# mLSTM head norm as a per-chunk factor and offset on ScalarE, and the first convolution tap on ScalarE

## The chip, the cores and the metric

The kernel runs on one core of one Trainium2 chip. The metric is the device time of one execution in microseconds (us); lower is better. A core has five engines with a queue each: PE (TensorE, matrix products), DVE (VectorE), ACT (ScalarE), POOL (GpSimd) and SP (SyncE, which here only issues transfers). Each engine takes its queue strictly in order, and an instruction that waits holds up everything behind it.

## The reference, cut to what matters

One layer over 1024 tokens of width 1024: differential attention and an mLSTM side by side, sigmoid gates, a gated MLP, a final norm. The change lies in the mLSTM branch, four heads of 128 channels:

```python
qk_m = jax.nn.silu(causal_dwconv(qk_m, conv_m_w[i]))           # 4 taps per channel
qm, km = jnp.split(qk_m, 2, axis=-1)
...
h = num / jnp.maximum(jnp.abs(den), jnp.exp(-m_t))[..., None]   # mLSTM output per token
...
def head_layernorm(x, g):
    mu = jnp.mean(xf, axis=-1, keepdims=True)
    var = jnp.mean(jnp.square(xf - mu), axis=-1, keepdims=True)
    return (xf - mu) * lax.rsqrt(var + EPS) * g
hm = head_layernorm(hm, ml_norm_g[i]) * jax.nn.sigmoid(om)
```

## The kernel before, in words

Features lie on the 128 partitions and tokens in the free dimension, except inside an mLSTM head, where tokens are on partitions. Float32 accuracy comes from splitting each operand into a high and a low part (`split`, L119 to L126: ACT writes `wh`, DVE writes `wl`), so each product is three matmuls of 128x512 (L374, L375, L376).

The large projections run as pairs through `products` (L366): seven blocks, in the order B11, T1, T2, B21, T3, B22, T4, of 12 matmuls each. Three PSUM banks serve a pair: b2 takes B11, T2, T3 and T4, b3 takes T1 and B22, b4 takes B21. `c_blocks` (L787) copies the bank after B11, T1 and T2 to SBUF on ACT (`copy`, L295) and adds in the later blocks on DVE (`tt`, L292). So T3 may not write b2 before ACT has copied T2's sum out of it (the copy named `u2`).

The stage of the mLSTM heads alternates pairs of projections with the work of a head:

- `make_qk(h)` (L800) computes query and key of a head and runs the four-tap convolution per half of 512 tokens in `conv_silu` (L804): the first tap on DVE (L807), three more taps by DVE (L810, and L813 for the few columns that reach into the other half), a sigmoid on ACT (L816), a product on DVE (L292 or L820).
- `mlstm_head(h)` (L855) forms scores (`pS`, L877) and transposed keys (`pk`, L878) from query and key, multiplies by decay weights on DVE (`xb`, L292, and `kw`, L880), and steps through eight chunks of 128 tokens: `pn` (L888, L890) into `num` by ACT (L891), and the state `C` by `pc` (L894) and DVE (L899).
- The head norm then works on `num`, 128 partitions x 8 chunks x 128 channels (a 129th column is the denominator): `rd` is the reciprocal of the denominator (L907 to L909), `mu` minus the mean (L910, L911). Three DVE passes over all 1024 columns add `mu` (L912), multiply by `rd` (L915) and multiply by the root (L921). Between them ACT squares each chunk and sums it (L918, an activation and a read of the accumulator per chunk), DVE scales the sums (L919) and POOL raises them to the power of minus a half (L920).
- `mlstm_out` (L925) runs the next pair of projections (`gate_pair`) and transposes `num` on PE (`pt`, L932, eight matmuls), which DVE multiplies into the output gate (`om`, L934). After the last head, SP loads the outputs of heads 0 to 2 back (`hml`, L541) and ACT and DVE split them.

The order of the instructions on each engine's queue is not that of the code: when the program is built, a scheduler places them by its own estimates of cost. The heads' work is therefore mixed with the products of the pairs, and a changed instruction can move others.

Of the kernel before, what the change touches and what calls it, by code (L numbers as in the profile page):

```python
# [13 lines left out]
AF = mybir.ActivationFunctionType  # L14
ALU = mybir.AluOpType
# [4 lines left out]
P = 128  # L20
# [4 lines left out]
NTB = S // P  # L25
# [44 lines left out]
def block_kernel(ctx: ExitStack, tc: tile.TileContext, a: dict, out: bass.AP):  # L70
    nc = tc.nc
    PE, ACT, DVE, POOL, SP = nc.tensor, nc.scalar, nc.vector, nc.gpsimd, nc.sync
# [25 lines left out]
    def v(name, i=0, n=1):  # L98
        lo = _VEC_COLS[name][0] + i
        return vec[:, lo:lo + n]  # L100

    def acc(name):
        return pools["acc"].tile([P, HALF], F32, tag="acc", name=name)

    def mid(name):
        if "mid" not in pools:
            return acc(name)
        return pools["mid"].tile([P, HALF], F32, tag="mid", name=name)
# [4 lines left out]
    def half_slice(half):  # L113
        return slice(half * HALF, (half + 1) * HALF)
# [81 lines left out]
    with tc.tile_pool(name="ld", bufs=3) as ld:  # L196

        ss = [ld.tile([P, S], F32, tag=f"ss{q}", name="ss1", bufs=1) for q in range(2)]
        for k in range(KD):
# [10 lines left out]
            else:  # L210
                DVE.tensor_scalar(out=hi, in0=xt, scalar1=v("g1", k), scalar2=None, op0=ALU.mult)
            DVE.scalar_tensor_tensor(out=lo, in0=xt, scalar=v("g1", k), in1=hi.bitcast(F32),
                                     op0=ALU.mult, op1=ALU.subtract)
# [77 lines left out]
    def tt(eng, out, in0, in1, op):  # L291
        eng.tensor_tensor(out=out, in0=in0, in1=in1, op=op)  # L292

    def copy(out, ps):
        ACT.activation(out=out, in_=ps, func=AF.Copy)  # L295
# [485 lines left out]
    def work(name, w=S, dtype=F32):  # L781
        return mw.tile([P, w], dtype, tag="m", name=name)

    def s_tile(tag, bufs=1):
        return mw.tile([P, HALF], F32, tag=tag, name=tag, bufs=bufs)

    def c_blocks(blocks, ready):  # L787

        s1, u2, s5 = s_tile("s1"), s_tile("u2"), s_tile("s5")
        for blk, ps in products(blocks):  # L790
            if blk in ("B11", "T1", "T2"):
                copy({"B11": s1, "T1": s5, "T2": u2}[blk], ps)
            elif blk == "T4":
                ready(1, 0, ps)
            else:
                t, row, half = {"B21": (s1, 0, 0), "T3": (s5, 1, 1), "B22": (u2, 0, 1)}[blk]
                tt(DVE, t, ps, t, ALU.add)
                ready(row, half, t)

    def make_qk(h):  # L800
        cvs = [mw.tile([P, S], F32, tag="cv", name="cv", bufs=3) for _ in range(2)]
        z = {}

        def conv_silu(row, half, prev):  # L804
            o, zt = cvs[row][:, half_slice(half)], z[row, half]
            i = h + 4 * row
            DVE.tensor_scalar(out=o, in0=zt, scalar1=v("cm", i * 4 + 3), scalar2=None, op0=ALU.mult)  # L807
            for j in (2, 1, 0):
                d, w = 3 - j, v("cm", i * 4 + j)
                DVE.scalar_tensor_tensor(out=o[:, d:], in0=zt[:, :HALF - d], scalar=w, in1=o[:, d:],  # L810
                                         op0=ALU.mult, op1=ALU.add)
                if half:
                    DVE.scalar_tensor_tensor(out=o[:, :d], in0=prev[:, HALF - d:], scalar=w, in1=o[:, :d],  # L813
                                             op0=ALU.mult, op1=ALU.add)
            sg = s_tile("sg", 2)
            ACT.activation(out=sg, in_=o, func=AF.Sigmoid)  # L816
            if row == 0:
                tt(DVE, o, o, sg, ALU.mult)
            else:
                DVE.scalar_tensor_tensor(out=o, in0=o, scalar=P ** -0.5, in1=sg, op0=ALU.mult, op1=ALU.mult)  # L820

        def ready(row, half, t):
            z[row, half] = t
            if row == 0:
                conv_silu(row, half, z[0, 0])
            elif half == 0:
                c21 = z[1, 0] = s_tile("c")
                copy(c21, t)
                conv_silu(1, 0, None)
                conv_silu(1, 1, c21)  # L830

        c_blocks(zb, ready)
        return cvs
# [21 lines left out]
    def mlstm_head(h):  # L855
        v1 = v1s[h]
        qT, kT = qks[h]
        g = slice(h * 8, h * 8 + 8)

        wb = work("wb")  # L860
        SP.dma_start(out=wb, in_=bc_d[1, g, :].rearrange("c t -> (c t)").partition_broadcast(P))
        dec = mw.tile([P, NTB], F32, tag="dec", name="dec", bufs=2)
        DVE.tensor_copy(out=dec, in_=wb.rearrange("p (c t) -> p c t", c=NTB)[:, :, P - 1])
        DVE.tensor_tensor(out=wb, in0=wb, in1=qT, op=ALU.mult)
        xb = work("xb")
        SP.dma_start(out=xb, in_=bc_d[0, g, :].rearrange("c t -> (c t)").partition_broadcast(P))
        xv = xb.rearrange("p (c t) -> p c t", c=NTB)
        DVE.tensor_tensor(out=xv, in0=xv, in1=mask.unsqueeze(1).to_broadcast([P, NTB, P]), op=ALU.add)
        for c in range(NTB):
            ACT.activation(out=xv[:, c, :], in_=xv[:, c, :], func=AF.Exp, bias=mg[:, 0, h * 8 + c:h * 8 + c + 1])  # L870
        kw = work("kw")
        for half in range(2):
            hs = half_slice(half)
            pS, pk = acc("pS"), acc("pk")
            for c in range(4):
                cs, cg = slice(c * P, (c + 1) * P), slice((4 * half + c) * P, (4 * half + c + 1) * P)
                PE.matmul(pS[:, cs], kT[:, cg], qT[:, cg], start=True, stop=True)  # L877
                PE.transpose(pk[:, cs], kT[:, cg], ident)  # L878
            tt(DVE, xb[:, hs], pS, xb[:, hs], ALU.mult)
            DVE.tensor_tensor(  # L880
                out=kw[:, hs].rearrange("p (c d) -> p c d", c=4), in0=pk.rearrange("p (c d) -> p c d", c=4),
                in1=mg[:, 1, h * 8 + 4 * half:h * 8 + 4 * half + 4].unsqueeze(2).to_broadcast([P, 4, P]), op=ALU.mult)
        num = work("num", NTB * (P + 1)).rearrange("p (c e) -> p c e", c=NTB)
        C = None
        for c in range(NTB):
            cs = slice(c * P, (c + 1) * P)
            pn = mid("pn")
            PE.matmul(pn[:, :P + 1], xb[:, cs], v1[:, c, :], start=True, stop=(c == 0))  # L888
            if c:
                PE.matmul(pn[:, :P + 1], wb[:, cs], C, start=False, stop=True)  # L890
            ACT.activation(out=num[:, c, :], in_=pn[:, :P + 1], func=AF.Copy)  # L891
            if c < NTB - 1:
                pc = mid("pc")
                PE.matmul(pc[:, :P + 1], kw[:, cs], v1[:, c, :], start=True, stop=True)  # L894
                Cn = mw.tile([P, P + 1], F32, tag="C", name="C", bufs=2)
                if c == 0:
                    DVE.tensor_copy(out=Cn, in_=pc[:, :P + 1])
                else:
                    DVE.scalar_tensor_tensor(out=Cn, in0=C, scalar=dec[:, c:c + 1], in1=pc[:, :P + 1],  # L899
                                             op0=ALU.mult, op1=ALU.add)  # L900
                C = Cn

        def col(name):
            return mw.tile([P, NTB], F32, tag=name, name=name, bufs=2)

        rd, mu, var = col("rd"), col("mu"), col("var")
        DVE.scalar_tensor_tensor(out=rd, in0=num[:, :, P], scalar=-1.0, in1=num[:, :, P], op0=ALU.mult, op1=ALU.max)  # L907
        DVE.tensor_tensor(out=rd, in0=rd, in1=mg[:, 2, g], op=ALU.max)
        DVE.reciprocal(out=rd, in_=rd)  # L909
        DVE.tensor_reduce(out=mu, in_=num[:, :, 0:P], axis=AX.X, op=ALU.add)  # L910
        DVE.tensor_scalar(out=mu, in0=mu, scalar1=-1.0 / P, scalar2=None, op0=ALU.mult)  # L911
        DVE.tensor_tensor(out=num[:, :, 0:P], in0=num[:, :, 0:P],  # L912
                          in1=mu.unsqueeze(2).to_broadcast([P, NTB, P]), op=ALU.add)

        DVE.tensor_tensor(out=num[:, :, 0:P], in0=num[:, :, 0:P],  # L915
                           in1=rd.unsqueeze(2).to_broadcast([P, NTB, P]), op=ALU.mult)
        for c in range(NTB):
            ACT.activation(out=xb[:, c * P:(c + 1) * P], in_=num[:, c, 0:P], func=AF.Square, accum_out=var[:, c:c + 1])  # L918
        DVE.tensor_scalar(out=var, in0=var, scalar1=1.0 / P, scalar2=EPS, op0=ALU.mult, op1=ALU.add)  # L919
        POOL.tensor_tensor(out=var, in0=var, in1=mhalf, op=ALU.pow)  # L920
        DVE.tensor_tensor(out=num[:, :, 0:P], in0=num[:, :, 0:P],  # L921
                           in1=var.unsqueeze(2).to_broadcast([P, NTB, P]), op=ALU.mult)
        return num

    def mlstm_out(h, num):  # L925
# [15 lines left out]
    for h in range(H):  # L941
        num = mlstm_head(h)
# [27 lines left out]
    for n, j in enumerate(OUT_ORDER):  # L970
        i = j % 4
# [249 lines left out]
    with tc.tile_pool(name="fin", bufs=2) as fp:  # L1221
# [25 lines left out]
        for t0, t1 in PLE_CHUNKS:  # L1247
            n = t1 - t0
            c = slice(t0, t1)
# [109 lines left out]
```

## Time and profile before

| | before |
|---|---|
| median of 3 runs | 1614.94 us (1612.32 to 1615.09) |
| profiled execution, its own time | 1610.4 us |
| span of its instructions | 1608.6 us |
| PE busy | 1548.1 us, 96% of the span |
| DVE busy | 1238.0 us, 77% |
| ACT busy | 718.9 us, 45% |
| POOL busy | 23.4 us, 1% |

Durations are read from the profiled execution. Its time is 4.5 us below the median, of which 1.8 us lie outside the span of its instructions. PE's share is not the share of a peak: matmuls overlap, and a start follows the one before by less than the duration shown.

### The profile page before, as it was taken

The numbers are of one execution on the slowest core, as the hardware profiler recorded it, in microseconds if no ns is written. First come the engines' busy times: TensorE is split into PE (matmuls) and PEld (weight loads), VectorE is DVE, ScalarE is ACT, GpSimd is POOL, SyncE is SP. The second block draws the span as 40 slices with busy tenths as digits, with TensorE's granted clock in tenths as the row PEclk, the third lists the DMA queues.
The fourth block names the chain that finished last, engine by engine and source line by source line (L and its number), as shares of the span: only waits on it lengthen the run. The fifth ranks groups of instructions, "written<-read, shape, count | busy, mean of one in ns | idle before, by whom it ended". The sixth has DMA issues, their size and how long they took to land.

```text
span 1608.6 us, 21129 instructions
## 1 busy us (share of the span) xinstructions
PE 1548.1 (96%) x7413; PEld 1274.6 (79%) x7413; DVE 1238.0 (77%) x2176; ACT 718.9 (45%) x1396; POOL 23.4 (1%) x22
## 2 busy tenths in 40 slices
PE   8999999989999999998998999999999989999997
PEld 6777877768778888786876888888888778788997
DVE  6687675596887878679869877787888887878745
ACT  3354553455466474443446433333333634344522
POOL 0000000000000000000000000000000000000000
PEclk9999999999999999999999999999999989999999
DMA  5212121163324232555223333333333745342422
GB/s 188 74 53 60 53 61 34 54 228 120 125 92 151 92 99 79 180 181 166 102 79 112 126 104 99 105 105 100 104 101 103 256 140 168 123 130 59 135 84 92
DMA packets 97882, 181.62 MB, mean 113 GB/s; under 512 B 11696, under 2 KB 21488, under 8 KB 97776
## 3 DMA queue, kind: packets, MB, share of 16 engines
q1 hardware_dynamic: 97200, 179.76, 34.6%
q8 instruction: 58, 0.95, 0.3%
q10 hardware_dynamic: 576, 0.52, 0.1%
q14 instruction: 48, 0.39, 0.1%
HBM read 131.18 MB, written 44.86 MB: 109 GB/s over the span
## 4 chain that ended last, share of the span: by engine, by line
PE 63%; DVE 10%; DMA 3%; issue 3%; ACT 1%; POOL 0%; SPq 0%; POOLq 0%; DVEq 0%; ACTq 0%
PE b L376 18%; PE b L374 17%; PE b L375 17%; PE ps_pg L1259 2%; PE ps_pg L1260 2%; PE ps_pg L1261 1%; DVE T L122 1%; DVE cv L810 1%; DVE mg L292 1%; DVE wl L122 1%; DVE B L122 1%; PE ps_ya L152 1%; DVE hs L388 1%; PE ps_ya L151 1%; PE ps_ya L150 1%
## 5 line engine op out<-in xcount | busy, mean ns | idle before, releaser
L376 PE MATMUL b<-T,wl 128*128 128x512 f32 x816 | 320.2, 392 | 5.1 <-DVE wl L122 5.1
L374 PE MATMUL b<-T,wh 128*128 128x512 f32 x816 | 320.0, 392 | 4.4 <-ACT s L295 1.8
L375 PE MATMUL b<-T,wh 128*128 128x512 f32 x816 | 319.2, 391 | 0.5 <-DVE T L122 0.5
L121 ACT ACTIVATE wh<-S 128x512 fp32r<-128x512 f32 (+1 forms) x208 | 129.4, 622 | 272.7 <-PE b L375 249.5
L374 PE MATMUL b<-B,wh 128*128 128x512 f32 x612 | 240.5, 393 | 2.3 <-ACT wh L121 1.8
L376 PE MATMUL b<-B,wl 128*128 128x512 f32 x612 | 239.7, 392 | 1.3 <-DVE wl L122 1.3
L375 PE MATMUL b<-B,wh 128*128 128x512 f32 x612 | 239.3, 391 | 1.1 <-DVE B L122 1.1
L122 DVE TENSOR_TENSOR wl<-S,wh 128x512 fp32r<-128x512 f32 (+1 forms) x208 | 140.0, 674 | 60.0 <-ACT wh L121 59.9
L374 PEld LDWEIGHTS b<-T,wh 128*128 128x128 f32 x816 | 154.0, 189 | 39.9 <-DVE x L292 2.4
L376 PEld LDWEIGHTS b<-T,wl 128*128 128x128 f32 x816 | 154.0, 189 | 39.3 <-DVE wl L122 7.3
L375 PEld LDWEIGHTS b<-T,wh 128*128 128x128 f32 x816 | 154.0, 189 | 33.6 <-DVE T L122 1.6
L121 ACT ACTIVATE wh<-wr 128x512 fp32r<-128x512 f32 (+1 forms) x156 | 96.9, 621 | 166.8 <-PE b L375 151.6
L374 PEld LDWEIGHTS b<-B,wh 128*128 128x128 f32 x612 | 115.2, 188 | 27.6 <-ACT wh L121 3.1
L376 PEld LDWEIGHTS b<-B,wl 128*128 128x128 f32 x612 | 115.2, 188 | 26.2 <-DVE wl L122 2.5
L375 PEld LDWEIGHTS b<-B,wh 128*128 128x128 f32 x612 | 115.2, 188 | 25.5 <-DVE B L122 2.1
L292 DVE TENSOR_TENSOR x<-b,x 128x512 f32<-128x512 f32 x112 | 77.0, 687 | 48.9 <-PE b L376 46.7
L122 DVE TENSOR_TENSOR wl<-wr,wh 128x512 fp32r<-128x512 f32 (+1 forms) x156 | 104.9, 672 | 7.5 <-ACT wh L121 7.3
L292 DVE TENSOR_TENSOR S<-wr 128x512 f32<-128x512 f32 (+1 forms) x104 | 70.3, 676 | 2.8 <-DMA wr<-w_o 0.7
L1104 DVE SCALAR_TENSOR_TENSOR ac<-ar,vec,ac 128x511 f32<-128x511 f32 (+1 forms) x88 | 65.7, 747 | 0.7
L649 ACT ACTIVATE e<-ps_s,nmax 128x128 f32<-128x128 f32 (+7 forms) x64 | 47.1, 737 | 35.9 <-DVE nmax L668 21.9
L1259 PE MATMUL ps_pg<-x,wpg 128*128 128x384 f32 (+1 forms) x192 | 61.3, 319 | 0.0
L1261 PE MATMUL ps_pg<-x,wpg 128*128 128x384 f32 (+1 forms) x192 | 61.0, 318 | 0.0
(303 smaller groups left out, 2725.1 us busy)
## 6 DMA issues: line engine op xcount, KB each, us to landing
wr<-w_up SPq DMA_DIRECT2D x88, 256.0 KB, 2.9
wr<-w_in SPq DMA_DIRECT2D x56, 256.0 KB, 3.0
wf<-w_in SPq DMA_DIRECT2D x32, 256.0 KB, 2.9
wr<-w_down SPq DMA_DIRECT2D x32, 256.0 KB, 2.9
xt<-xT SPq DMA_DIRECT2D x8, 512.0 KB, 7.0
sw<-raw SPq DMA_DIRECT2D x64, 64.0 KB, 2.0
hs<-xT SPq DMA_DIRECT2D x8, 512.0 KB, 5.3
ya<-ya SPq DMA_DIRECT2D x16, 256.0 KB, 2.0
```

The source lines that it names most:

```text
L121: ACT.activation(out=hi, in_=src, func=AF.Copy)
L122: (lo_eng or DVE).tensor_tensor(out=lo, in0=src, in1=hi.bitcast(F32), op=ALU.subtract)
L150: PE.matmul(ps, wh, xh, start=(first and k == 0), stop=False)
L292: eng.tensor_tensor(out=out, in0=in0, in1=in1, op=op)
L374: PE.matmul(bank[b], wh, xh, start=(k == 0 and not more), stop=False, **kw)
L375: PE.matmul(bank[b], wh, xl, start=False, stop=False, **kw)
L376: PE.matmul(bank[b], wl, xh, start=False, stop=(k == n - 1), **kw)
L649: ACT.activation(out=e, in_=s_, func=AF.Exp, bias=nm[:, m:m + 1], scale=1.0, accum_out=rs[:, m:m + 1])
L1104: DVE.scalar_tensor_tensor(out=o[:, d:], in0=ar[:, j + d:j + HALF], scalar=v("cf", t * 3 + j), in1=o[:, d:], op0=ALU.mult, op1=ALU.add)
L1259: PE.matmul(pg, wh, xh[:, c], start=(i == 0), stop=False)
L1260: PE.matmul(pg, wh, xl[:, c], start=False, stop=False)
L1261: PE.matmul(pg, wl, xh[:, c], start=False, stop=(i == KD - 1))
```

## The change

For each chunk, mean, denominator and root become one factor and one offset per token. `mu` is now minus the mean times the reciprocal denominator (one small DVE instruction, L912 of the changed file). ACT's Square takes `rd` as scale and `mu` as bias (L914), and after the power on POOL two small DVE multiplies put the root into both. A second pass of ACT over the eight chunks, an Identity with the factor as scale and the offset as bias (L921), writes the normalised `num`. The three DVE passes over 1024 columns are gone. In the convolution the first tap of each half is now a Copy with scale on ACT.

```diff
         def conv_silu(row, half, prev):
             o, zt = cvs[row][:, half_slice(half)], z[row, half]
             i = h + 4 * row
-            DVE.tensor_scalar(out=o, in0=zt, scalar1=v("cm", i * 4 + 3), scalar2=None, op0=ALU.mult)
+            ACT.activation(out=o, in_=zt, func=AF.Copy, scale=v("cm", i * 4 + 3))
             for j in (2, 1, 0):
...
         DVE.tensor_reduce(out=mu, in_=num[:, :, 0:P], axis=AX.X, op=ALU.add)
-        DVE.tensor_scalar(out=mu, in0=mu, scalar1=-1.0 / P, scalar2=None, op0=ALU.mult)
-        DVE.tensor_tensor(out=num[:, :, 0:P], in0=num[:, :, 0:P],
-                          in1=mu.unsqueeze(2).to_broadcast([P, NTB, P]), op=ALU.add)
-
-        DVE.tensor_tensor(out=num[:, :, 0:P], in0=num[:, :, 0:P],
-                           in1=rd.unsqueeze(2).to_broadcast([P, NTB, P]), op=ALU.mult)
+
+        DVE.scalar_tensor_tensor(out=mu, in0=mu, scalar=-1.0 / P, in1=rd, op0=ALU.mult, op1=ALU.mult)
         for c in range(NTB):
-            ACT.activation(out=xb[:, c * P:(c + 1) * P], in_=num[:, c, 0:P], func=AF.Square, accum_out=var[:, c:c + 1])
+            ACT.activation(out=xb[:, c * P:(c + 1) * P], in_=num[:, c, 0:P], func=AF.Square,
+                           scale=rd[:, c:c + 1], bias=mu[:, c:c + 1], accum_out=var[:, c:c + 1])
         DVE.tensor_scalar(out=var, in0=var, scalar1=1.0 / P, scalar2=EPS, op0=ALU.mult, op1=ALU.add)
         POOL.tensor_tensor(out=var, in0=var, in1=mhalf, op=ALU.pow)
-        DVE.tensor_tensor(out=num[:, :, 0:P], in0=num[:, :, 0:P],
-                           in1=var.unsqueeze(2).to_broadcast([P, NTB, P]), op=ALU.mult)
+        tt(DVE, rd, rd, var, ALU.mult)
+        tt(DVE, mu, mu, var, ALU.mult)
+        for c in range(NTB):
+            ACT.activation(out=num[:, c, 0:P], in_=num[:, c, 0:P], func=AF.Identity,
+                           scale=rd[:, c:c + 1], bias=mu[:, c:c + 1])
         return num
```

The scheduler also moves instructions. On PE, the transposes of `num` in the first head's gate pair stood after the last of T4's products, before the next pair began:

```order
L374 MATMUL b_4078<-T_3583,wh 128x512
L375 MATMUL b_4078<-T_3583,wh 128x512
L376 MATMUL b_4078<-T_3583,wl 128x512
L932 MATMUL pt<-ident,num 128x128 x8
L374 MATMUL b_4247<-B_3201,wh 128x512
```

In the changed program (where bank b2 of this pair is b_4085 and b4 is b_4087) they stand after the last of B21's products, before T3:

```order
L374 MATMUL b_4087<-B_3383,wh 128x512
L375 MATMUL b_4087<-B_3383,wh 128x512
L376 MATMUL b_4087<-B_3383,wl 128x512
L932 MATMUL pt<-ident,num 128x128 x8
L374 MATMUL b_4085<-T_3387,wh 128x512
```

The transposes moved up by three blocks, 36 matmuls; it is so in all four heads.

On ACT, the same place before (L891 evicts `num`, L295 copies a bank after B11, T1 and T2, L121 is the split of the weights):

```order
L891 ACTIVATE num<-pn 128x129 x8
L121 ACTIVATE wh<-wr 128x512
L295 ACTIVATE s_4075<-b_4078 128x512
L121 ACTIVATE wh<-S_4115 128x512
L295 ACTIVATE s_4077<-b_4079 128x512
L918 ACTIVATE xb,var<-num 128x128 x8
L295 ACTIVATE u_4076<-b_4078 128x512
L121 ACTIVATE wh<-S_4134 128x512
```

And in the changed program:

```order
L891 ACTIVATE num<-pn 128x129 x8
L121 ACTIVATE wh<-wr 128x512
L295 ACTIVATE s_4082<-b_4085 128x512
L914 ACTIVATE xb,var<-num,mu,rd 128x128 x8
L295 ACTIVATE s_4084<-b_4086 128x512
L121 ACTIVATE wh<-S_4122 128x512
L921 ACTIVATE num<-num,mu,rd 128x128 x8
L295 ACTIVATE u_4083<-b_4085 128x512
L121 ACTIVATE wh<-S_4141 128x512
```

The copy of T2's sum out of bank b2 (`u`) now stands behind both passes over the chunks, the Squares and the Identities.

On SP, after the last head, the transfers before (`wr` are weights, `hml` the stored outputs of heads 0 to 2, `ga` and `gb` stores of gates):

```order
L841 DMA gb_377<-c 128x512
L327 DMA wr<-w_in 128x512 x2
L541 DMA hml<-hm_355 128x512 x2
L541 DMA hml<-hm_356 128x512 x2
L541 DMA hml<-hm_357 128x512
L841 DMA ga_369<-s_5940 128x512
```

And in the changed program:

```order
L841 DMA gb_377<-c 128x512
L327 DMA wr<-w_in 128x512
L541 DMA hml<-hm_355 128x512 x2
L541 DMA hml<-hm_356 128x512 x2
L541 DMA hml<-hm_357 128x512 x2
L327 DMA wr<-w_in 128x512
L841 DMA ga_369<-s_5968 128x512
```

One of the two weight loads that stood ahead of the six loads of `hml` now stands behind them.

## Rows read from the trace of the kernel before

**Rows 1.** The page: busy time by engine.
```profile
PE 1548.1 (96%) x7413; PEld 1274.6 (79%) x7413; DVE 1238.0 (77%) x2176; ACT 718.9 (45%) x1396; POOL 23.4 (1%) x22
```
**Rows 2.** What PE waited for, 390 to 670 us: total us, times, longest.
```profile
PE pS L877 <- DVE cv L820: 4.5, 3, 1.5
PE pS L877 <- issue: 2.3, 1, 2.3
PE b L374 <- ACT s L295: 1.8, 1, 1.8
PE pc L894 <- DVE kw L880: 0.6, 2, 0.3
```
**Rows 3.** Timeline of DVE, convolution of head 1: start us, us, instruction.
```profile
460.94 0.69 DVE L292 TENSOR_TENSOR s<-b,s 128x512 f32<-128x512 f32 x1 [0.86 <-PE b L376]
...
462.15 0.48 DVE L807 TENSOR_SCALAR cv<-s,vec 128x512 f32<-128x512 f32 x1
462.66 1.54 DVE L810 SCALAR_TENSOR_TENSOR cv<-s,vec,cv 128x511 f32<-128x511 f32 x2
...
468.25 0.48 DVE L807 TENSOR_SCALAR cv<-u,vec 128x512 f32<-128x512 f32 x1
468.64 0.68 DVE L122 TENSOR_TENSOR wl<-S,wh 128x512 fp32r<-128x512 f32 x1
```
**Rows 4.** Timeline of PE, the same place: the scores of head 1.
```profile
476.92 1.16 PE L877 MATMUL pS<-cv 128*128 128x128 f32 x8 [1.51 <-DVE cv L820]
```
**Rows 5.** Groups of ACT's instructions: busy us, mean ns, idle before.
```profile
L295 ACT ACTIVATE s<-b 128x512 f32<-128x512 f32 x72 | 42.1, 584 | 1.0 <-DVE cv L810 0.9
...
L870 ACT ACTIVATE xb<-xb,mg 128x128 f32<-128x128 f32 x32 | 10.9, 392 | 0.6 <-DVE xb L868 0.5
...
L918 ACT ACTIVATE xb<-num 128x128 f32<-128x128 f32 x32 | 9.4, 297 | 1.3 <-DVE num L915 1.3
...
L627 ACT ACTIVATE oh<-po,vec 128x512 f32<-128x512 f32 x8 | 5.5, 683 | 6.4 <-PE po L625 6.3
```
**Rows 6.** Timeline of DVE, norm of head 0.
```profile
433.88 0.20 DVE L909 RECIPROCAL rd<-rd 128x8 f32<-128x8 f32 x1
...
434.54 1.22 DVE L912 TENSOR_TENSOR num<-num,mu 128x1024 f32<-128x1024 f32 x1
...
439.59 0.17 DVE L919 TENSOR_SCALAR var<-var 128x8 f32<-128x8 f32 x1 [0.24 <-ACT xb L918]
441.65 1.22 DVE L921 TENSOR_TENSOR num<-num,var 128x1024 f32<-128x1024 f32 x1 [1.89 <-POOL var L920]
```
**Rows 7.** Timeline of ACT, norm of head 0.
```profile
437.11 0.31 ACT L918 ACTIVATE xb<-num 128x128 f32<-128x128 f32 x1 [0.68 <-DVE num L915]
437.32 0.19 ACT L918 ACTIVATION_READ_ACCUMULATOR xb<-num 128x1 f32 x1
...
439.46 0.58 ACT L295 ACTIVATE u<-b 128x512 f32<-128x512 f32 x1
```
**Rows 8.** Timeline of PE, gate pair of head 0: B11 ends, T1 begins, transposes.
```profile
432.36 0.39 PE L376 MATMUL b<-B,wl 128*128 128x512 f32 x1
432.59 0.40 PE L374 MATMUL b<-T,wh 128*128 128x512 f32 x1
...
448.97 1.03 PE L932 MATMUL pt<-ident,num 128*128 128x128 f32 x8
```
**Rows 9.** Transfers issued by SP after the last head.
```profile
638.93 8.61 SPq L327 DMA_DIRECT2D wr<-w_in  x2
647.59 2.32 SPq L541 DMA_DIRECT2D hml<-hm  x5
```
**Rows 10.** Busy time by stretch; after the five engines, the granted clock (PEclk), DMA share, GB/s.
```profile
405.00:409.50 4.50, 2.18 (x15) 1.67 (x13) 4.50 (x10) 2.49 (x4) 0.00 (x0) 1.00 0.00 0
734.00:738.70 4.70, 0.61 (x3) 0.17 (x1) 4.70 (x9) 1.23 (x2) 0.00 (x0) 1.00 0.36 113
738.90:742.10 3.20, 3.02 (x7) 2.47 (x8) 3.20 (x7) 1.26 (x2) 0.00 (x0) 0.50 0.00 0
```

## The prediction

> **What bounds the kernel now.** I read the busy times first, then PE's waits in the stage of the heads, then timelines of the places that the change touches. PE is busy 96% of the span, DVE 77%, ACT 45% [rows 1]: work taken from DVE pays only where PE waits for DVE, and work given to ACT costs only where PE comes to wait for ACT. Between 390 and 670 us PE waits in few places [rows 2]: four times at the scores, L877, for the last product of the convolution on DVE (4.5 us in three heads, 2.3 us in the first, where the row says issue); twice at the state update for `kw`, 0.6 us in all; once, after the last head, 1.8 us for a copy by ACT. For the head norm it does not wait at all: the transposes of head 0 run at 448.97 [rows 8], while DVE's last pass over `num` starts at 441.65 and takes 1.22 [rows 6], so it was done 6 us earlier.
>
> **The convolution: -4.6 us.** Head 1 stands for the four. DVE is handed the third block at 460.94 [rows 3] and works without a pause until PE can start the scores at 476.92 [rows 4]. A first tap holds DVE's queue for 0.51 us once (462.15 to 462.66) and for 0.39 in the other places (468.25 to 468.64) [rows 3]; four per head are 1.7 us less. Given back: one narrow instruction (L813, some 0.13 us) now stands ahead of the last product; and the first tap's result now comes from ACT. ACT can begin only when DVE's addition ends at 461.63, and needs about 0.7 us: a copy of 512 columns takes 0.584 and one with a scale per partition 0.683 [rows 5]. So DVE's second tap starts at about 462.5 instead of 462.15, a loss of 0.35. The other three taps are covered by other DVE work: from 462.66 on DVE has some 14 us of passes of its own, and ACT needs 0.7 for each tap; the sigmoid behind them adds 0.1. Net 1.7 - 0.13 - 0.35 - 0.1 = 1.1 to 1.2 us per head, 4.6 in four. All of it is on the path, as the waits were 1.5 and 2.3 us long. Bounds: 3.4, if every tap but one must be waited for as the first, and 6.8, if none is.
>
> **Scores and keys: +1.2 us.** The changed order puts the fourth score product of the first half and its DVE multiplication (0.68 us, the size of the addition of rows 3) late, just ahead of `kw`. `kw` then comes up to 0.6 us later, and PE waits for it where the row says 0.6 us in all [rows 2]. One or two products that now stand between cover a part. I take 0.3 us per head; bounds 0 and 0.6.
>
> **The head norm: +12.1 us.** This is the largest term, and it comes from the moved transposes. In head 0's own clock before: the reciprocal ends at 434.08 [rows 6]; the new small product (0.17, like L919) ends at 434.3; ACT's Squares start at 434.4 instead of 437.11 [rows 7], as L912 and L915 are gone. A Square and its accumulator read took (439.46 - 437.11) / 8 = 0.294 us, of which the Square held the queue for 0.21 [rows 7]. The new Square has two operands per partition, `rd` and `mu`. Rows show what one such operand costs: L870, an Exp with a bias per partition, takes 392 ns against 297 for L918 of the same size, and L627, a Copy with a scale per partition, 683 against 584 for L295 [rows 5]; 95 to 99 ns each. No row has two. Bounds: they share one 95 ns, or each costs 95. Scale alone and bias alone cost the same, so I take 190 ns. Eight Squares then take 8 x 0.484 = 3.9 us, to 438.25; DVE's L919 starts 0.13 later, as it did; from its start to the end of POOL's power 2.06 us pass (439.59 to 441.65) [rows 6]; two small multiplies bring us to 440.75. Eight Identities at 0.20 + 0.19 us end at 443.85.
>
> The Trainium skill, page ScalarE: Activation LUTs, section What ACT_TABLE_LOAD costs, says that each such pointer operand adds about 93 ns to an ACTIVATE. By it the sum is the one forecast here, by the shared end it would be some 8 us smaller; no run so far shows two operands.
>
> Now PE. T1 of this pair started at 432.59, behind five products of B11; three remain there in the changed order, so T1 starts 0.45 earlier, at 432.14. Three blocks of 12 matmuls at 0.23 (432.36 to 432.59 [rows 8]) bring PE to the transposes at 440.3. They need 0.8 us, so T3 could start at 441.1. But the transposes need the Identities, and T3 needs the copy `u` out of bank b2, which on ACT stands behind the Identities and takes 0.58 [rows 7]: it ends at 444.43. PE loses 3.3 us. In heads 2 and 3 six products of B11 remain behind the last state product, before and after, so PE arrives 0.55 us later against the norm and loses 2.75. Two of each: 12.1 us. With operands sharing one 95 ns, 16 instructions are 1.5 us shorter per head, so 6.0 us; with operands that cost nothing, about 0.3 us.
>
> **After the last head: -1.8 us.** The wait for ACT's copy there [rows 2] came from the queue: SP sat 8.6 us on two weight loads before the loads of `hml` went out at 647.59 [rows 9], and DVE and ACT stood waiting for these. Now one weight load stands ahead of them, and DVE is held up by the norm some 3 us less. I take the whole wait as gone; bound: nothing gained.
>
> **The clock: +1.6 us.** After 4.5 us of waiting at 734 the granted clock fell to half, from 1.00 to 0.50, and seven matmuls passed in 3.2 us, where 14 pass at 0.23 [rows 10]: some 1.6 us lost. After the 2.3 us wait of head 0 (405.00 to 409.50) it stayed at 1.00. The new waits lie between, and eight transposes break them up. I count one fall; bounds none and four.
>
> **What is hidden.** The table loads are as many as before. ACT gets some 28 us more over the stage; outside the waits named it is covered by ACT's idle time before its splits. DVE's other savings, some 14 us of passes over `num`, end in DVE waiting for PE.
>
> **The sum.** -4.6 + 1.2 + 12.1 - 1.8 + 1.6 = +8.5 us. Against the profiled execution, 1610.4, that is 1618.9; the median of the runs lies 4.5 us higher, at 1614.94, so I forecast 1623.4 us.
>
> **The rivals.**
> *The operands share their cost.* The norm term is 6.0 and the clock stays: -4.6 + 1.2 + 6.0 - 1.8 = +0.8, 1615.7 us. For it: no row with two. Against it: scale and bias cost the same one by one. Chance 0.16.
> *The norm arrives in time, and the convolution decides: faster.* If extra operands cost nothing in a row of ACTIVATEs, the Identities and the copy end about when PE arrives: -4.6 + 1.2 + 0.3 - 1.8 = -4.9, 1610.0 us. The point at which it turns: the eight Squares and eight Identities together must take under some 4.5 us, where I expect 7. Against it: L870 in a row of eight kept its 392 ns. Chance 0.09.
> *The clock falls in every head.* The waits of 2.75 to 3.3 us lie above the one that did no harm: four falls, +4.8 more, and with `kw` at its upper bound 1629.4 us. Against it: the transposes run within the wait. Chance 0.15.
>
> **How the numbers follow.** The forecast has 0.60. A measurement can tell about 0.2%, 3.2 us. Slower: the forecast and the last rival, less what errors of the small terms take away, 0.72. Same: most of the first rival, and those errors, 0.18. Faster: the second rival, 0.10. The range goes from 1611, just above the second rival, to 1630, which takes in four falls; a tenth is left out at each end. Within it the forecast alone spans 1619 to 1628 (two terms off by their half bounds).
>
> **What would show it.** Right: DVE without L807, and PE's wait at L877 down to about 0.5 us (1.3 in head 0); Squares near 480 ns; PE idle before L932 and the T3 behind it, released by ACT's Identity and its copy of `u`, about 3 us per head; the wait after the last head gone. Wrong: Squares near 390 ns or less, PE passing L932 without a wait, or L877 waiting as long as before, now for ACT.

## The result and the profile after

| | before | after |
|---|---|---|
| median of 5 runs | 1614.94 us (1608.49 to 1615.24) | 1622.1 us (1617.8 to 1624.87) |
| ratio | | 1.0054, 95% interval 1.004 to 1.0068 |
| profiled execution | 1610.4 us | 1623.04 us |

The change makes the kernel slower: 0.54% of 1614.94 is 8.7 us, by the interval 6.5 to 11.0. The ratio is taken over all runs; the two medians differ by 7.2 us. The forecast was +8.5 us and 1623.4.

Busy time by engine, on the page of the changed kernel:

```profile
PE 1562.8 (96%) x7413; PEld 1278.1 (79%) x7413; DVE 1219.6 (75%) x2156; ACT 747.1 (46%) x1444; POOL 23.4 (1%) x22
```

Against [rows 1], DVE has 18 us less and ACT 28 us more, as the code says. PE has 14.7 us more with the same 7413 matmuls, which is no new work. Of this, 13.2 us arise in the stage of the heads: about 8 us at the transposes, where part of PE's waiting is recorded as busy, and most of the rest in products at half clock; both are shown below.

What PE waited for in the stage of the heads, after (total us, times, longest):

```profile
PE pt L932 <- ACT num L921: 1.4, 2, 0.8
PE pS L877 <- DVE cv L820: 0.8, 3, 0.3
PE pS L877 <- issue: 0.8, 1, 0.8
PE b L374 <- ACT u L295: 0.5, 3, 0.2
PE pk L878 <- ACT c L850: 0.2, 1, 0.2
PE pn L888 <- DVE xb L292: 0.2, 1, 0.2
```

Read against [rows 2], the waits have fallen from 9.2 us to 3.9, and the kernel got slower. The timeline of PE in the gate pair of head 0 shows what this view leaves out:

```profile
438.28 0.39 PE L376 MATMUL b<-B,wl 128*128 128x512 f32 x1
439.45 3.02 PE L932 MATMUL pt<-ident,num 128*128 128x128 f32 x8 [0.78 <-ACT num L921]
442.63 0.50 PE L374 MATMUL b<-T,wh 128*128 128x512 f32 x1 [0.15 <-ACT u L295]
```

From the start of the first transpose to the end of the last pass 3.02 us, where it was 1.03 [rows 8]. The timeline of ACT for the same time gives the reason (the first and last of the eight Squares, and the second pass):

```profile
432.54 0.49 ACT L914 ACTIVATE xb<-num,mu,rd 128x128 f32<-128x128 f32 x1 [1.06 <-DVE mu L912]
...
435.90 0.48 ACT L914 ACTIVATE xb<-num,mu,rd 128x128 f32<-128x128 f32 x1
436.29 0.19 ACT L914 ACTIVATION_READ_ACCUMULATOR xb<-num,mu,rd 128x1 f32 x1
436.38 0.58 ACT L295 ACTIVATE s<-b 128x512 f32<-128x512 f32 x1
436.86 0.62 ACT L121 ACTIVATE wh<-S 128x512 fp32r<-128x512 f32 x1
438.91 3.19 ACT L921 ACTIVATE num<-num,mu,rd 128x128 f32<-128x128 f32 x8 [1.43 <-DVE mu L292]
442.00 0.57 ACT L295 ACTIVATE u<-b 128x512 f32<-128x512 f32 x1
```

Each transpose follows one Identity, at the Identities' pace of (442.00 - 438.91) / 8 = 0.386 us. One transpose is now recorded with 0.33 us, where it was 0.27 with a start every 0.11; so only 0.06 us of each step shows as idle, too short to be listed as a wait, and 2.63 of the 3.02 us count as busy. From the last product of B21 to the first of T3 PE needs 442.63 - 438.28 = 4.35 us. Without a wait one product and eight transposes take 1.02: in the kernel before, the last product of T4 starts at 448.74 and the next product behind the transposes at 449.76. ACT itself stands idle for 1.43 us ahead of the Identities, with the copy `u` queued behind them.

To see all of the loss I take the starts of successive matmuls from the timeline of PE and compare each step with what the same step takes without a wait (0.227 us for 512 columns, 0.23 in [rows 8]). Between the same two matmuls, 60 ahead of head 0's first score and the first product of the stage after the heads, 301.63 us pass before and 310.89 after: +9.26. The forecast's terms are on its own scale in this table:

| term | forecast us | measured us |
|---|---|---|
| waits at the scores (convolution) | -4.6 | -5.3 |
| scores, keys and state | +1.2 | +0.9 |
| transposes and the T3 behind them (norm) | +12.1 | +11.7 |
| after the last head | -1.8 | -2.0 |
| clock | +1.6 | +4.0 |
| sum | +8.5 | +9.3 |

The two profiled executions differ by more, 12.6 us. The further 3.4 us arise outside the stage of the heads, most of them at about 850 to 900 and 1290 us, where the order of the instructions is the same on all engines; the runs, with +8.7 us, give no ground to count them to the change, and what causes them is not shown.

### The profile page after: what moved, and what is told of

It is laid out like the page before. It is cut to its first block, busy times and chain, and to the rows that moved or that the text cites. A ratio compares the mean times of both kernels' runs of the same rounds, so it can differ in the third digit from the quotient of the medians.

```text
span 1621.2 us, 21139 instructions
## 1 busy us (share of the span) xinstructions
PE 1562.8 (96%) x7413; PEld 1278.1 (79%) x7413; DVE 1219.6 (75%) x2156; ACT 747.1 (46%) x1444; POOL 23.4 (1%) x22
## 4 chain that ended last, share of the span: by engine, by line
PE 48%; DVE 6%; DMA 2%; issue 2%; ACT 1%; POOL 0%; SPq 0%; POOLq 0%; DVEq 0%; ACTq 0%
PE b L374 14%; PE b L376 14%; PE b L375 14%; PE ps_pg L1259 1%; PE ps_pg L1261 1%; PE ps_pg L1260 1%; DVE T L122 1%; DVE mg L292 1%; DVE B L122 1%; DVE wl L122 1%; DVE S L292 0%; DVE hs L388 0%; DMA x<-xT 0%; DMA B<-gd5B 0%; DMA T<-gd1T 0%
## 5 line engine op out<-in xcount | busy, mean ns | idle before, releaser
L121 ACT ACTIVATE wh<-S 128x512 fp32r<-128x512 f32 (+1 forms) x208 | 129.2, 621 | 254.2 <-PE b L375 226.3
L121 ACT ACTIVATE wh<-wr 128x512 fp32r<-128x512 f32 (+1 forms) x156 | 96.9, 621 | 159.6 <-PE b L375 143.2
```

The lines of the kernel that those rows point to most:

```text
L121: ACT.activation(out=hi, in_=src, func=AF.Copy)
```

## The experiments

Ratios stand against the kernel before, run on the same chip; "stage" is the time between the same two matmuls as above, against 301.63 us, in the profiled execution.

| version | ratio (95% interval) | stage us |
|---|---|---|
| the change | 1.0054 (1.004 to 1.0068) | +9.3 |
| first tap alone | 0.9963 (0.9947 to 0.998) | -1.9 |
| norm alone | 1.0062 (1.0045 to 1.0079) | +11.7 |
| late second pass | 0.9969 (0.9953 to 0.9986) | -4.5 |
| one operand | 1.0004 (0.9986 to 1.0021) | +0.4 |
| transposes held back | 1.0116 (1.0097 to 1.0135) | +17.8 |
| copy first | 0.9996 (0.9981 to 1.0012) | -1.8 |
| late second pass, three taps | 0.9983 (0.9969 to 0.9996) | not comparable, the scores lie elsewhere |

### The first tap alone

```diff
-            DVE.tensor_scalar(out=o, in0=zt, scalar1=v("cm", i * 4 + 3), scalar2=None, op0=ALU.mult)
+            ACT.activation(out=o, in_=zt, func=AF.Copy, scale=v("cm", i * 4 + 3))
```

> The first tap alone on ACT; the norm as before. My theory (the terms of the change add up, and the taps are the gain): the four waits at the scores shrink by 5.3 us in all, as in the changed kernel, the later score product gives back 0.9, everything else stays: about 4.4 us faster than before, a ratio near 0.997, and PE's wait for ACT's copy after the last head (2.0 us) is still there. Rival A (the change is slow because ACT has too much work, wherever it stands): the taps cost too, ratio 1.000 or above.

Measured: 0.9963, some 6 us faster. PE's waits, 390 to 680 us:

```profile
PE b L374 <- ACT s L295: 1.6, 1, 1.6
PE pS L877 <- issue: 1.4, 1, 1.4
PE pS L877 <- DVE cv L820: 0.8, 3, 0.3
```

The waits at the scores shrink from 6.8 us to 2.2, and the one after the last head stays. The profiled execution shows only 1.9 us in the stage. Of the 4 us between this and the runs, 1.6 are one fall of the clock behind that last wait, which did not come before (eight products at half pace); the rest is not explained. The taps are a gain; rival A falls.

### The norm alone

The changed kernel with its first line of the diff undone (the tap on DVE).

> The norm alone as in the change; first tap on DVE as before. My theory: PE's waits at the transposes cost 11.7 us as in the changed kernel, clock falls behind them up to 4 us, and the wait after the last head (2.0 us) goes: 9.7 to 13.7 us slower than before, a ratio of 1.006 to 1.0085; the waits at the scores are as before. Rival A (ACT's load as such): a smaller part, since only some of the added work is here; about 1.003.

Measured: 1.0062, 10 us slower; stage +11.7. The waits:

```profile
PE pS L877 <- DVE cv L820: 4.6, 3, 1.5
PE pS L877 <- issue: 1.7, 1, 1.7
PE pc L894 <- DVE kw L880: 1.2, 2, 1.0
PE pt L932 <- ACT num L921: 0.6, 2, 0.4
PE b L374 <- ACT u L295: 0.5, 3, 0.2
```

Scores as before, nothing after the last head; the steps around the transposes lose 10.9 us where the change loses 11.7, and the clock falls in two heads. All that is lost comes with the norm. In the stage the two halves add up to the change (-1.9 and +11.7 against +9.3). In the runs they do so only roughly: 0.9963 x 1.0062 is 1.0025, where the change has 1.0054; the cause of this gap is open.

### The second pass emitted late

ACT runs the same activations as in the change. Only the place of the loop in the code differs, and the scheduler then puts `u` ahead of it on ACT and the transposes behind T4 on PE. One thing more differs: ACT loads its tables 16 times instead of 22 (1.28 us each).

```diff
         gate_pair(T_OM + h, T_GA + h, om)
+        for c in range(NTB):
+            ACT.activation(out=num[:, c, 0:P], in_=num[:, c, 0:P], func=AF.Identity,
+                           scale=rd[:, c:c + 1], bias=mu[:, c:c + 1])
         for half in range(2):
```

(The same loop is taken out of `mlstm_head`.)

> The whole change, but the second pass of ACT is emitted behind the products of the gate pair, so that the copy of T2's sum stands ahead of it on ACT and the transposes stand behind T4 on PE, as before the change. ACT does exactly the work of the change. My theory (the place of the pass, not its work, costs the time): the 11.7 us at the transposes go, and the clock falls with them; left are the taps' 5.3 us of gain less 0.9; the wait of 2.0 us after the last head may come back, since SP's order there is that of before: about 4.4 us faster than before, a ratio near 0.997. Rival A (ACT's load as such): as slow as the change, 1.005.

Measured: 0.9969, 5 us faster; stage -4.5. ACT's timeline at head 0:

```profile
437.22 0.62 ACT L121 ACTIVATE wh<-S 128x512 fp32r<-128x512 f32 x1
437.74 0.58 ACT L295 ACTIVATE u<-b 128x512 f32<-128x512 f32 x1
438.22 0.63 ACT L121 ACTIVATE wh<-S 128x512 fp32r<-128x512 f32 x1
439.28 0.49 ACT L927 ACTIVATE num<-num,mu,rd 128x128 f32<-128x128 f32 x1 [0.43 <-DVE mu L292]
```

The copy and a split run in the time in which ACT waited for the power in the change, 437.74 against 442.00. PE's waits:

```profile
PE pS L877 <- issue: 0.9, 1, 0.9
PE pS L877 <- DVE cv L820: 0.8, 3, 0.3
PE b L376 <- DVE wl L122: 0.5, 2, 0.3
PE b L374 <- ACT s L295: 0.4, 1, 0.4
PE pk L878 <- ACT c L850: 0.2, 1, 0.2
```

Nothing is left at the transposes. So the second pass costs PE nothing there when it stands late; its early place costs the 11.7 us. A new wait of 0.5 us, for the `wl` of DVE's split, is small beside that. The six table loads that are saved do not explain this: in the change no table load lies between the Squares and `u`, so none is part of the wait. What is gained against the kernel before comes from the taps: with the norm unchanged they gave 0.9963, and 0.9969 is no better. Moving the norm to ACT, even well placed, shows no gain of its own in the runs. One thing I had not expected: the wait after the last head is 0.4 us and not 1.8 [rows 2], although SP's order there is the old one.

### One operand per activation

```diff
-                           scale=rd[:, c:c + 1], bias=mu[:, c:c + 1], accum_out=var[:, c:c + 1])
+                           bias=mu[:, c:c + 1], accum_out=var[:, c:c + 1])
...
-                           scale=rd[:, c:c + 1], bias=mu[:, c:c + 1])
+                           scale=rd[:, c:c + 1])
```

> The whole change, but the Square keeps only its bias per partition and the Identity only its scale per partition: one operand each, so the statistics and the mean's part of the result are left out. My theory (each operand costs 95 ns, and the 16 activations are in the path): Square and Identity take about 392 ns, some 1.5 us less per head, so PE's loss at the transposes falls from 11.7 to about 5.7 us; with clock falls as before them 6 us faster than the change, without falls 10: between 1 us faster and 3 us slower than before, a ratio of 0.9995 to 1.002. Rival B (the operands do not set the wait; the queue order or POOL's power does): the same loss at the transposes as the change, ratio 1.005.

Measured: 1.0004; stage +0.4. The groups of ACT in the changed kernel, and then with one operand (busy us, mean ns, idle before):

```profile
L914 ACT ACTIVATE xb<-num,mu,rd 128x128 f32<-128x128 f32 x32 | 15.4, 482 | 3.0 <-DVE mu L912 3.0
...
L921 ACT ACTIVATE num<-num,mu,rd 128x128 f32<-128x128 f32 x32 | 12.8, 481 | 5.4 <-DVE mu L292 5.4
```

```profile
L914 ACT ACTIVATE xb<-num,mu 128x128 f32<-128x128 f32 x32 | 12.4, 389 | 3.0 <-DVE dec L863 2.1 <-DVE mu L912 0.9
L921 ACT ACTIVATE num<-num,rd 128x128 f32<-128x128 f32 x32 | 9.8, 390 | 5.3 <-DVE mu L292 5.3
```

With the Square before the change, 297 ns [rows 5], this is a ladder: no operand 297, one 389, two 482. The loss at the transposes and T3 falls from 11.7 to 7.2 us, by 4.5 where I expected 6, and no clock fall follows. The scheduler also moved transposes behind T4 in this version: one of eight in heads 0 and 1, six of eight in heads 2 and 3. The time from the last product of B21 to the first of T3 is set by `u` all the same. It is 2.78, 2.63, 2.22 and 2.10 us in the four heads, where the change needs 4.35, 4.18, 3.63 and 3.63: 1.4 to 1.6 us less in each, and sixteen operands at 93 ns are 1.5. Rival B falls.

### The transposes held back, ACT's order as in the change

```diff
+        id2 = mw.tile([P, P], F32, tag="id2", name="id2", bufs=1)
+        DVE.scalar_tensor_tensor(out=id2, in0=t4[:, 0:P], scalar=0.0, in1=ident, op0=ALU.mult, op1=ALU.add)
...
-                PE.transpose(pt[:, i * P:(i + 1) * P], num[:, half * 4 + i, 0:P], ident)
+                PE.transpose(pt[:, i * P:(i + 1) * P], num[:, half * 4 + i, 0:P], id2)
```

(`t4` is the tile that the gate of T4 is written to.)

> The whole change with ACT's order as in the change (both passes ahead of the copy of T2's sum), but the transposes held back on PE until T4 has been read: they take an identity that DVE writes after T4's gate. My theory (T3 needs the copy, and the copy stands behind the Identities, so the place of the transposes is not what holds PE): PE now waits at T3 itself for ACT's copy, from its arrival to the copy's end, about 4.1, 3.9, 3.4 and 3.4 us in the four heads, 15 us in all where the change has 11.7 net at the transposes; the clock falls behind most of these unbroken waits: ratio 1.006 to 1.009, no faster than the change. Rival C (the early transposes alone cost the time): the waits go, as in the version with the late pass, ratio 0.997.

Measured: 1.0116, the slowest of all. The first of PE's waits:

```profile
PE b L374 <- ACT u L295: 14.7, 4, 4.3
```

The four waits, 3.9, 4.3, 3.3 and 3.3 us, are near the forecast; the ratio is above the expected range, a miss, since the clock fell in every head, in two of them before the wait had ended. In the windows by stretch (the five engines, then the granted clock), the first wait and the stretches behind the four waits:

```profile
439.00:443.00 4.00, 0.15 (x1) 0.00 (x0) 2.14 (x5) 3.64 (x10) 0.00 (x0) 0.80 0.00 0
443.10:447.90 4.80, 4.80 (x11) 3.78 (x12) 1.99 (x3) 3.17 (x5) 0.00 (x0) 0.50 0.32 105
517.80:523.10 5.30, 5.30 (x13) 4.15 (x14) 1.99 (x3) 3.34 (x6) 0.00 (x0) 0.50 0.28 99
591.90:594.80 2.90, 2.90 (x8) 2.27 (x7) 1.30 (x3) 2.00 (x3) 0.00 (x0) 0.50 0.34 116
663.60:666.50 2.90, 2.90 (x8) 2.30 (x7) 1.54 (x3) 0.56 (x2) 0.00 (x0) 0.50 0.25 88
```

At half clock a product starts every 0.43 us instead of 0.23; the steps above 0.23 add up to 7.7 us over the four. The early transposes alone are therefore not the cause: they even filled part of the wait that T3 has for `u`. Rival C falls.

### The copy first, the transposes among T3's products

The second pass and the transposes are emitted between B21 and T3. ACT copies `u` first, and PE does the transposes one by one with products of T3 between them.

> The whole change, but the second pass and the transposes are emitted between B21 and T3: the copy of T2's sum stands ahead of the Identities on ACT, and the transposes lie singly among the products of T3 on PE. My theory (the copy's place on ACT is half of the loss, and T3's products can fill the time between two Identities): PE loses about 1 us per head where the change loses 2.9 net, few clock falls: -5.3 + 0.9 + 4 and up to 2 for the wait after the last head gone or not, some -2 to +1 us against before, ratio 0.998 to 1.001. Rival C (early transposes cost the time wherever the copy is): as slow as the change, 1.005.

Measured: 0.9996; stage -1.8. PE's wait for the Identities:

```profile
PE pt L936 <- ACT num L931: 1.6, 4, 0.6
```

All the steps of PE around the transposes lose some 5 us in four heads, where I expected 4 and the change loses 11.7, and the clock does not fall in the stage. So early transposes cost less than half as much once `u` is out of the bank, as T3's products then fill the time between two Identities.

### The late second pass, with the very first tap back on DVE

```diff
-            ACT.activation(out=o, in_=zt, func=AF.Copy, scale=v("cm", i * 4 + 3))
+            if (row, half) != (0, 0):
+                ACT.activation(out=o, in_=zt, func=AF.Copy, scale=v("cm", i * 4 + 3))
+            else:
+                DVE.tensor_scalar(out=o, in0=zt, scalar1=v("cm", i * 4 + 3), scalar2=None, op0=ALU.mult)
```

> The version with the late second pass, with the very first tap of a head back on DVE and the other three on ACT. The changed kernel let DVE stand 0.19 us for the first tap, against 0.51 us that the tap takes on DVE, so by DVE's time alone this costs 0.3 us a head. But the built order puts all scores later on PE, behind one more block of products, so that PE should not wait for them at all (2.4 us less), while the head's chain ends later. My theory: 0 to 2 us faster than the version with the late pass, ratio to before 0.995 to 0.997. Rival D (the later chain makes PE wait for the state update or the norm): no faster than before, 1.000 or above.

Measured: 0.9983, a miss, between my range and that of rival D: no better than the late pass with all four taps, whose interval overlaps this one. The waits at the scores are gone, as the order said, but PE now waits elsewhere:

```profile
PE b L376 <- DVE wl L122: 2.6, 4, 0.8
PE pn L891 <- DVE xb L292: 0.3, 1, 0.3
```

A place later on PE only moved the wait from the scores to the weights that DVE splits behind the convolution. The profiled execution was the fastest of its 12 runs (1604.87 us, median 1609.43), so it can't show where the median lies.

## Why the prediction was right, point by point

**The norm (+12.1 forecast, +11.7 measured).** The mechanism is the one forecast: the Identities and the copy `u` behind them set T3. By head the loss is 3.3, 3.2, 2.6 and 2.6 us, where 3.3 and 2.75 were forecast, twice each. The version with the late pass takes the loss away with the same activations, and the one with held-back transposes shows that T3 itself waits for `u`. The operands cost what was taken: 482 ns for two, where 190 ns on top of 297 were reckoned. From DVE's scaling of the sums to the first use of POOL's power the same 2.06 us passed, 436.51 to 438.57 in head 0. The Trainium skill, page ScalarE: Activation LUTs, section What ACT_TABLE_LOAD costs, gives about 93 ns for each such operand; the runs show 92 for the first and 93 for the second. What I did not foresee is the form: PE does not stand still and then transpose, but transposes at the pace of the Identities, so the list of waits shows 1.9 us of a loss of 11.7.

**The convolution (-4.6, -5.3).** Right in place and kind. DVE stood less for the first tap than the 0.35 us taken, as the timeline of DVE in head 1 shows after the change:

```profile
462.62 0.68 DVE L122 TENSOR_TENSOR wl<-wr,wh 128x512 fp32r<-128x512 f32 x1
463.49 1.54 DVE L810 SCALAR_TENSOR_TENSOR cv<-s,vec,cv 128x511 f32<-128x511 f32 x2 [0.19 <-ACT cv L807]
```

It is 0.19, and so in all four heads; 0.16 us less in each is most of the difference between -4.6 and -5.3. The tap on ACT took 710 to 726 ns, near the 0.7 us reckoned. The lower bound of 3.4 does not follow from its condition: three waits of 0.35 us in a head leave some 0.4 us, 1.7 in four heads.

**Scores and keys (+1.2, +0.9).** The list has no wait for `kw` any more, where I had it grow; small waits of the transposed keys (`pk`, for a gate on ACT) and of `pn` took its place. The size was near by luck, the row was wrong.

**After the last head (-1.8, -2.0).** Gone, as forecast, but the cause I put first, SP's order, is not needed for most of it: the late version has SP's old order and DVE relieved of its passes, and waits 0.4 us there; the taps alone, with the old order and the old passes, keep 1.6. These two versions differ in all of the norm, so that it was DVE's passes is likely but not shown.

**The clock (+1.6, +4.0).** The term of the sum that was mis-sized. I counted one fall, because the new waits are shorter than the one at 734 us and transposes lie in them. There were three in four heads. The windows of the changed kernel, where the transposes of heads 0 to 3 run or have just run:

```profile
439.50:442.50 3.00, 2.59 (x8) 1.06 (x8) 1.24 (x2) 3.00 (x9) 0.00 (x0) 1.00 0.00 0
512.50:515.50 3.00, 3.00 (x8) 2.08 (x8) 1.60 (x3) 2.98 (x6) 0.00 (x0) 0.50 0.00 0
584.00:587.00 3.00, 3.00 (x7) 2.41 (x8) 2.55 (x4) 2.97 (x5) 0.00 (x0) 0.50 0.12 46
656.00:659.00 3.00, 3.00 (x8) 2.32 (x7) 2.15 (x4) 0.60 (x2) 0.00 (x0) 0.50 0.08 18
```

In heads 1 to 3 the granted clock is half, though PE had done a transpose every 0.39 us. Head 0, with as long a row of spaced transposes, kept the full clock in this execution. The norm alone fell in heads 0 and 2. So more than one head falls in both versions, and which ones these rows do not tell. That the sum came so near is in part luck: the clock cost 2.4 us more than forecast, and the other terms together 1.6 less, +5.3 against +6.9.

**The rivals.** "The operands share their cost" and "the norm arrives in time" fall with the ladder of 297, 389 and 482 ns. "The clock falls in every head" was nearer to the truth than its chance of 0.15: three of four.

## What to carry to other kernels

Before moving work to an idle engine, look at what stands behind it in that engine's queue: here 3 us of second pass cost PE its wait mostly because a copy that frees a PSUM bank was queued behind it, and emitting the same loop later in the code turned 1.0054 into 0.9969. Test the parts of a change one by one as well: the tap alone gave 0.9963, so the norm's move could be left out. Count two per-partition operands as twice the price of one (92 and 93 ns here, on 128x128 tiles). And when a kernel gets slower while its waits shrink, compare the busy time of the bound engine at an equal number of instructions: waits that are shared out between instructions hide there.

## What the runs showed of the hardware

A matmul that waits a little can be recorded as busy for part of it: eight transposes, each waiting for its Identity, stand with 0.33 us and a start every 0.39, where they had 0.27 and a start every 0.11; this is about 8 of the 14.7 us by which PE's busy time rose with the same 7413 matmuls. A per-partition operand of an ACTIVATE of 128x128 float32 cost 92 ns, a second one 93 more. A thin row of transposes, one per 0.39 us, did not keep the granted clock at 1.00 in three of four heads. With each of the four unbroken waits of 3.3 to 4.3 us in the version with held-back transposes a fall came, within the wait or less than 1 us behind it. The length of a wait alone does not tell: after the last head the clock stayed at 1.00 behind a wait of 1.8 us in the kernel before, and fell behind one of 1.6 us in the version with the taps alone.
